# First feed-forward product of a decoder layer, by 2x2x2 blocks with seven products in fifteen of its sixteen column groups

## The chip, the cores and the metric

The kernel runs on one NeuronCore of a Trainium2 chip. The metric is the time of one execution on the device in microseconds (us). The engines are named as the profile names them: PE is TensorE's matrix multiply, PEld its loading of the stationary operand, DVE is VectorE, ACT is ScalarE, POOL is GpSimd, and SP only issues transfers here. POOL issues transfers too.

## What is computed

One decoder layer over 512 tokens of 2048 channels, in float32. Only the part around the change is kept here; the token mixers before it produce `mix`.

```python
x = layer_norm(DEEPNORM_ALPHA * x + mix, ln_mix_g, ln_mix_b)      # x: 512 x 2048
f = jnp.square(jax.nn.relu(x @ w_ff1)) @ w_ff2                    # w_ff1: 2048 x 8192, w_ff2: 8192 x 2048
x = layer_norm(DEEPNORM_ALPHA * x + f, ln_ff_g, ln_ff_b)
```

## The kernel before

**Three products for one.** Each float32 operand is split into a high and a low part of type fp32r, and each product is made of three: high by high, high by low and low by high. `split` does it with two instructions: ACT writes the high part (tile `wh` for weights), DVE writes source minus high part (tile `wl`). Where the split stands in a helper, all splits have its two lines, L86 (ACT) and L87 (DVE).

```python
    def split(dst_h, dst_l, src):                                        # L85
        nc.scalar.activation(dst_h, src, AF.Copy)                        # L86
        nc.vector.tensor_tensor(dst_l, src, dst_h.bitcast(F32), op=OP.subtract)
```

**Steps and their lead.** All products are a list of steps, each with one load of weights (tile `wr`, 512 KB by SP), one split and its matmuls. `fill(i)`, called ahead of the matmuls of step i, writes the loads and splits up to step i + 2 into the engines' programs. The tiles `wh` and `wl` have three buffers each, so the split of step i + 2 starts when step i - 1 has left PE: the splits lead PE by two steps. Every engine takes its instructions in the order in which the program writes them.

**The first feed-forward product (L146).** Its 8192 columns are done in 16 groups of 512. A group has 8 steps of 24 matmuls; the stationary operand is a 128x128 block of weights, the moving one 512 tokens of the activations (`aH`, `aL`), and four banks of PSUM (`mm`) collect the group. Group 0 is done in two halves of 256 tokens (`F[0]` and `F[1]`), since the second half of the tokens leaves the normalisation later; its 384 matmuls have 256 columns. The side work of the first groups finishes the normalised rows (`ln1_finish`, `y_save`) on DVE and ACT.

**What follows each group (`ff1_evac`, from L493).** ACT copies the four banks out with relu (L524) and squares them in place (L527) into `hpR`. Then `parts(0)` and `parts(1)`, one for each half of the group's tiles, are put into the list `late`, and the first and the second step of the next group take one each. A `parts` is: four sums on DVE (L498) that the second feed-forward product needs, a split of seven blocks into `hpH` (ACT) and `hpL` (DVE), and two transfers to HBM by POOL (`h_parts`, L503). The two `parts` of a group have buffers of their own (tags h1 to h6).

**The second feed-forward product (L615, L660)** reads `h_parts` back (`hop`) and already uses blocks of 2x2x2 with seven products. Its sums of weight blocks are on DVE (L585 to L596). The change leaves it as it is, except for the buffers that it starts with.

## Time and profile before

| | |
|---|---|
| Time, median of 3 runs (lowest to highest) | 2449.92 us (2448.81 to 2450.59) |
| Span of the profiled execution | 2448.5 us |
| PE, DVE, ACT, POOL busy, share of the span | 99%, 53%, 35%, 5% |
| Group 0 of the first feed-forward product, with normalisation work between its matmuls | 1110.0 to 1161.3 us |
| Groups 1 to 15 of the first feed-forward product | 1161.3 to 1814.2 us |
| Second feed-forward product and the end | 1814.2 us to the end |

The profiled execution has no time of its own beside its span; the median of the runs is 1.4 us above that span. Times in the trace count from the first instruction. In the rows below a group of instructions stands as line, engine, operation, output<-input, shape and count, then busy time, mean ns of one, and the idle time of the engine ahead of them with what ended it.

### The profile page before, as it was taken

To read this page: it belongs to the slowest core of one execution; us is meant where nothing else is said; L and a number is where in the kernel's file an instruction comes from. 1 tells how busy PE (TensorE), PEld (TensorE's weight loads), DVE (VectorE), ACT (ScalarE), POOL (GpSimd) and SP (SyncE) were. 2 spreads that over 40 slices of the span, in tenths; PEclk is the share of its full clock that TensorE was granted. 3 is DMA by queue.
4 is the path that set the end of the run, shared out by engine and by line. 5 is a ranking of instruction groups with operands and counts; after the bars stand their busy time and mean duration, and the time that the engine had idled before them with its cause. 6 is when DMAs were issued, how large, how long until landed. Compare 5 with 4: busy or idle time off the path is not lost.

```text
span 2448.5 us, 26732 instructions
## 1 busy us (share of the span) xinstructions
PE 2433.2 (99%) x10936; PEld 2010.9 (82%) x10936; DVE 1303.0 (53%) x1409; ACT 851.9 (35%) x952; POOL 130.7 (5%) x188
## 2 busy tenths in 40 slices
PE   9999999999999999999999999999999999999998
PEld 7888888877788888889888888888888888888886
DVE  4532245555522335356653334343347988889887
ACT  4323321244422222137434333343334333333330
POOL 0000000000000000000110101000021000110000
PEclk9999999999999999999999999999999999999999
DMA  6333333322233333465665645546677457575652
GB/s 217 87 94 99 103 96 95 95 78 78 71 93 97 101 95 116 125 198 167 195 243 166 217 155 196 183 160 210 241 262 261 160 186 240 206 240 168 210 164 94
DMA packets 166842, 383.29 MB, mean 157 GB/s; under 512 B 11200, under 2 KB 12224, under 8 KB 165696
## 3 DMA queue, kind: packets, MB, share of 16 engines
q1 hardware_dynamic: 133408, 257.84, 33.5%
q0 software_dynamic: 30720, 117.45, 13.8%
q10 hardware_dynamic: 2592, 6.29, 0.8%
q8 instruction: 86, 1.41, 0.2%
q14 instruction: 36, 0.29, 0.0%
HBM read 317.58 MB, written 63.96 MB: 156 GB/s over the span
## 4 chain that ended last, share of the span: by engine, by line
PE 97%; DVE 1%; DMA 1%; ACT 0%; issue 0%; SPq 0%; POOLq 0%; DVEq 0%
PE mm L146 71%; PE pp L615 20%; PE pp L660 4%; PE sc L349 1%; PE tp L381 1%; DMA w<-in_w_ff 1%; DVE wl L87 0%; PE tp L373 0%; PE tp L275 0%; PE sc L275 0%; DVE part L621 0%; DMA wr<-in_w_in 0%; PE sc L467 0%; PE tp L467 0%; ACT wh L86 0%
## 5 line engine op out<-in xcount | busy, mean ns | idle before, releaser
L87 DVE TENSOR_TENSOR wl<-wr,wh 128x1024 fp32r<-128x1024 f32 (+1 forms) x348 | 423.3, 1221 | 891.5 <-ACT wh L86 890.9
L146 PE MATMUL mm<-aH,wh 128*128 128x512 f32 (+1 forms) x1984 | 768.8, 387 | 0.8 <-ACT wh L86 0.6
L146 PE MATMUL mm<-aH,wl 128*128 128x512 f32 (+1 forms) x1984 | 759.4, 383 | 0.2 <-DVE wl L87 0.2
L146 PE MATMUL mm<-aL,wh 128*128 128x512 f32 (+1 forms) x1984 | 758.7, 382 | 0.0
L86 ACT ACTIVATE wh<-wr 128x1024 fp32r<-128x1024 f32 (+1 forms) x348 | 367.0, 1055 | 878.2 <-PE mm L146 809.0
L615 PE MATMUL pp<-wh,hop 128*128 128x512 f32 x1568 | 483.1, 389 | 0.7 <-ACT hpR L524 0.7
L146 PEld LDWEIGHTS mm<-aH,wh 128*128 128x128 f32 x1984 | 373.2, 188 | 76.4 <-ACT wh L86 2.3
L146 PEld LDWEIGHTS mm<-aL,wh 128*128 128x128 f32 x1984 | 373.2, 188 | 74.3 <-issue 1.9
L146 PEld LDWEIGHTS mm<-aH,wl 128*128 128x128 f32 x1984 | 373.0, 188 | 73.9 <-DVE wl L87 1.1
L615 PEld LDWEIGHTS pp<-wh,hop 128*128 128x128 f32 x1568 | 294.4, 188 | 62.0 <-ACT hpR L524 1.1
L86 ACT ACTIVATE wh<-w 128x1024 fp32r<-128x1024 f32 x196 | 208.1, 1062 | 313.6 <-PE pp L615 295.5
L615 PE MATMUL pp<-wl,hop 128*128 128x512 f32 x784 | 305.2, 389 | 1.0 <-DVE wl L87 1.0
L87 DVE TENSOR_TENSOR wl<-w,wh 128x1024 fp32r<-128x1024 f32 x196 | 238.4, 1222 | 71.4 <-ACT wh L86 64.3
L615 PEld LDWEIGHTS pp<-wl,hop 128*128 128x128 f32 x784 | 147.2, 188 | 32.4 <-DVE wl L87 1.9
L146 PE MATMUL mm<-wh,aH 128*128 128x512 f32 x384 | 149.9, 390 | 0.0
L146 PE MATMUL mm<-wl,aH 128*128 128x512 f32 x384 | 149.5, 389 | 0.0
L146 PE MATMUL mm<-wh,aL 128*128 128x512 f32 x384 | 149.5, 389 | 0.0
L621 DVE TENSOR_TENSOR part<-part,pp 128x1024 f32<-128x1024 f32 x92 | 112.1, 1218 | 12.7 <-PE pp L615 12.7
L87 DVE TENSOR_TENSOR hpL<-hpR,hpH 128x1792 fp32r<-128x1792 f32 (+1 forms) x30 | 61.3, 2044 | 52.1 <-ACT hpH L86 52.1
L146 PEld LDWEIGHTS mm<-wl,aH 128*128 128x128 f32 x384 | 72.1, 188 | 15.2 <-DVE wl L87 0.4
L146 PEld LDWEIGHTS mm<-wh,aL 128*128 128x128 f32 x384 | 72.1, 188 | 15.1
L146 PEld LDWEIGHTS mm<-wh,aH 128*128 128x128 f32 x384 | 72.1, 188 | 14.7
(143 smaller groups left out, 1700.1 us busy)
## 6 DMA issues: line engine op xcount, KB each, us to landing
wr<-in_w_ff SPq DMA_DIRECT2D x152, 512.0 KB, 3.9
wr<-in_w_in SPq DMA_DIRECT2D x127, 512.0 KB, 3.7
w<-in_w_ff SPq DMA_DIRECT2D x112, 512.0 KB, 6.1
hop<-h_parts POOLq DMA_DIRECT2D x98, 512.0 KB, 7.2
h_parts<-hpH POOLq DMA_DIRECT2D x28, 896.0 KB, 5.7
h_parts<-hpL POOLq DMA_DIRECT2D x28, 896.0 KB, 7.7
wr<-in_w_out SPq DMA_DIRECT2D x40, 512.0 KB, 3.7
wr<-in_w_branch_pool SPq DMA_DIRECT2D x16, 512.0 KB, 3.6
```

The lines of the kernel that those rows point to most:

```text
L86: nc.scalar.activation(dst_h, src, AF.Copy)
L87: nc.vector.tensor_tensor(dst_l, src, dst_h.bitcast(F32), op=OP.subtract)
L146: nc.tensor.matmul(o, l, r, start=first and j == 0, stop=last and j == 2)
L349: nc.tensor.matmul(p[:, :n], qT[h][:, qb * P:(qb + 1) * P], kT[h][:, :n], start=True, stop=True)
L381: nc.tensor.matmul(p[:, k * P:], vt["v"][:, k, h * HD:(h + 1) * HD], pT[h][:, k, k * P:], start=k == 0, stop=k == 3)
L615: nc.tensor.matmul(u.ps[:, t], l, r, start=q + j == 0, stop=q == 3 and j == 2)
L621: nc.vector.tensor_tensor(p, p, u.ps, op=OP.add)
L660: nc.tensor.matmul(o, l, r, start=first and i == 0, stop=last and i == 2)
```

## The change

Groups 1 to 15 are no longer steps of 512 tokens by 512 columns. Each is a unit (`FUnit`) of seven products of half the tokens (256), half the 2048 channels and half the 512 columns (M1 to M7), in the order M1 M2 M5 M3 M6 M7 M4, in group 1 M1 M5 M6 M3 M7 M2 M4. A product is two pieces (`FPiece`, numbered j = 0 to 13), a piece is one split of 128x1024 and 24 matmuls with 256 moving columns (L646). A unit has 14 pieces with 336 matmuls, where a group had 8 steps with 192. The split keeps its two instructions (now L89 and L90).

The weights of a unit are four blocks of 1 MB (`w1`), loaded by SP. Four times in a unit one block is added to another in place, 128x2048, on POOL (`W_ADD`, L608): after M1's split the block that M5 reads, after M5's those that M6 and M7 read, after M6's the one that M4 reads. The sums of the activations (`P1` to `P4`) are made once, by `y_sums` and `y_p3`, on DVE and ACT around the second half of group 0.

Three banks of PSUM serve a unit. M3 accumulates on M5's bank after M5's result has been copied out, M6 on M1's, M7 on the same bank after a copy of M1 + M6, and M4 on it after DVE has read it for a block. `hpR` and `hpH` have one buffer each. What followed a group (now `h_parts_out`) is still taken from `late` by the next unit's first two pieces. The finished normalised rows, before on DVE and ACT, are made by POOL in 16 chunks (`y_rows`): after piece 2 of units 1 to 9, and after piece 8 of units 1 to 7. The core of the diff:

```diff
+    W_ADD = nc.gpsimd.tensor_tensor
...
+            nc.gpsimd.dma_start(y_norm[t], acc[t])
...
+    def y_add(out, a, b, op):
+        nc.vector.tensor_tensor(yr[out], yr[a], yr[b], op=op)
+
+    def y_sum(name, src):
+        h = L2["p"].tile([P, 8, 256], F32R, name="ysH", tag=SUM[name][0])
+        l = L2["p"].tile([P, 8, 256], F32R, name="ysL", tag=SUM[name][1])
+        if name == "P2":
+            nc.scalar.activation(h, yr[src], AF.Copy, scale=-1.0)
+            nc.vector.scalar_tensor_tensor(l, yr[src], -1.0, h.bitcast(F32), op0=OP.mult, op1=OP.subtract)
+        else:
+            split(h, l, yr[src])
+        sums[name] = (h, l)
...
+    def y_sums():
+        return [lambda: (y_add("22", "22", "21", OP.subtract), y_sum("P1", "22")),
+                lambda: (y_add("21", "11", "21", OP.subtract), y_add("11", "11", "22", OP.add)),
+                lambda: (y_add("12", "11", "12", OP.subtract), y_sum("P2", "11")),
+                lambda: y_sum("P4", "12")]
...
+    def y_rows(t, n):
+        c = slice(n * 512, (n + 1) * 512)
+        v, g, b = low["u"][:, 1], low["g"][:, 0], low["g"][:, 1]
+        tt = nc.gpsimd.tensor_tensor
+        nc.gpsimd.dma_start(v, y_norm[t, :, c])
+        nc.gpsimd.dma_start(g, bcast(ln_mix_g, c))
+        nc.gpsimd.dma_start(b, bcast(ln_mix_b, c))
+        tt(v, v, g, op=OP.mult)
+        tt(v, v, b, op=OP.add)
+        nc.gpsimd.tensor_scalar(v, v, ALPHA, None, op0=OP.mult)
+        if t >= 2 and n % 2:
+            nc.gpsimd.dma_start(g, y_parts[t - 2, :, c])
+            tt(v, v, g, op=OP.subtract)
+        nc.gpsimd.dma_start(y_parts[t, :, c], v)
...
+    def h_parts_out(g, j):
+        r = R[g][:, j]
+        for d, x0, x1, op in ((4, 0, 2, OP.add), (5, 4, 1, OP.subtract), (6, 1, 0, OP.subtract), (7, 3, 5, OP.subtract)):
+            nc.vector.tensor_tensor(r[:, d], r[:, x0], r[:, x1], op=op)
+        h = L2["p"].tile([P, 7, 256], F32R, name="hpH", tag="t10")
+        split(h, r[:, 1:], r[:, 1:])
+        for e, v in enumerate((h.bitcast(F32), r[:, 1:])):
+            nc.gpsimd.dma_start(h_parts[g // 2, e, :, :, 2 * (g % 2) + j].rearrange("s p f -> p s f"), v)
...
-        def parts(j):
-            a, b, c = ("h1", "h2", "h3") if j else ("h4", "h5", "h6")
-            r = R[j]
-            for d, x0, x1, op in ((4, 0, 2, OP.add), (5, 4, 1, OP.subtract), (6, 1, 0, OP.subtract), (7, 3, 5, OP.subtract)):
-                nc.vector.tensor_tensor(r[:, d], r[:, x0], r[:, x1], op=op)
-            h = L2["p"].tile([P, 7, 256], F32R, name="hpH", tag=b)
-            l = L2["p"].tile([P, 7, 256], F32R, name="hpL", tag=c)
-            split(h, l, r[:, 1:])
-            for e, v in enumerate((h, l)):
-                nc.gpsimd.dma_start(h_parts[g // 2, e, :, :, 2 * (g % 2) + j].rearrange("s p f -> p s f"), v.bitcast(F32))
...
+    ORDER = ("M1", "M2", "M5", "M3", "M6", "M7", "M4")
+    ORDER1 = ("M1", "M5", "M6", "M3", "M7", "M2", "M4")
+    FACTORS = {"M1": ("11", "11"), "M5": ("P1", "11"), "M6": ("P2", "11"), "M3": ("P4", "22"), "M7": ("P3", "12"),
+               "M2": ("12", "21"), "M4": ("22", "11")}
...
+        def get(self, role):
+            self.b[role] = L2["p"].tile([P, 8, 256], F32, name="w1", tag=self.tag[role])
+            k, c0 = int(role[0]) - 1, self.g * 512 + (int(role[1]) - 1) * 256
+            nc.sync.dma_start(self.b[role], w_ff1[k * 1024:(k + 1) * 1024, c0:c0 + 256].rearrange("(a p) n -> p a n", p=P))
+
+        def sum(self, role, other):
+            W_ADD(self.b[role], self.b[role], self.b[other], op=OP.add)
+
+        def give(self, role, new):
+            self.next.tag[new] = self.tag[role]
+            self.next.get(new)
...
+        def split(self):
+            u, j, b = self.u, self.j, self.u.b
+            self.h = G.tile([P, 4, 256], F32R, name="wh", bufs=3)
+            self.l = G.tile([P, 4, 256], F32R, name="wl", bufs=3)
+            split(self.h, self.l, b[FACTORS[self.what][1]][:, 4 * (j % 2):4 * (j % 2) + 4])
+            if j % 2:
+                for o, i in {"M1": (("11", "12"),), "M5": (("11", "22"),), "M6": (("11", "21"),)}.get(self.what, ()):
+                    u.sum(o, i)
+            elif self.what == "M3":
+                u.sum("12", "22")
+            if j in (7, 9, 11, 13):
+                u.give(u.freed[j // 2 - 3], u.order[j // 2 - 3])
+
+        def mult(self):
+            u, what = self.u, self.what
+            if self.j % 2 == 0 and what in ("M1", "M5", "M2"):
+                u.ps[what] = PS.tile([P, 512], F32, name="mm", bufs=6)
+            p = u.ps[{"M3": "M5", "M2": "M2", "M5": "M5"}.get(what, "M1")]
+            for n in range(2):
+                o = p[:, n * 256:(n + 1) * 256]
+                for k in range(4):
+                    ah, al = yblock(FACTORS[what][0], 4 * (self.j % 2) + k)
+                    wh, wl = (v[:, k, n * P:(n + 1) * P] for v in (self.h, self.l))
+                    for i, (l, r) in enumerate(((wh, ah), (wh, al), (wl, ah))):
+                        first = what in ("M1", "M5", "M2") and self.j % 2 + n + k + i == 0
+                        nc.tensor.matmul(o, l, r, start=first, stop=self.j % 2 == 1 and k == 3 and i == 2,
+                                         skip_group_check=True)
+            if self.j % 2:
+                self.evac()
+
+        def evac(self):
+            u, what, ps = self.u, self.what, self.u.ps
+            v = {m: p.rearrange("p (n t) -> p n t", n=2) for m, p in ps.items()}
+            m1, m5, u2 = low["m"][:, 0], low["m"][:, 1], low["u"][:, 0]
+            tt, act = nc.vector.tensor_tensor, nc.scalar.activation
+
+            def block(slot, in0, in1, op):
+                r = R[u.g][:, :, slot]
+                tt(r, in0.rearrange("p (n t) -> p n t", n=2), in1, op=op)
+                act(r, r, AF.Relu)
+
+            if what == "M1":
+                act(m1, ps["M1"], AF.Copy)
+            elif what == "M5":
+                act(m5, ps["M5"], AF.Copy, scale=-1.0)
+            elif what == "M6":
+                act(u2, ps["M1"], AF.Copy, scale=-1.0)
+            elif what == "M3":
+                h_rows(u.g)
+            elif what == "M7":
+                block(3, m5, v["M1"], OP.subtract)
+            elif what == "M4":
+                act(R[u.g][:, :, 1], v["M1"], AF.Relu)
+                act(R[u.g][:, :, :4], R[u.g][:, :, :4], AF.Square)
+                late.extend(h_out(u.g))
+            if what == ("M2" if u.g == 1 else "M3"):
+                block(0, m1, v["M2"], OP.add)
+            if what == ("M3" if u.g == 1 else "M6"):
+                block(2, u2, v["M5"], OP.subtract)
...
-    F += [add(cols(w_ff1, n * 512), 16, "ws", yact, ff1_evac(n)) for n in range(1, 16)]
+    funits = [FUnit(g) for g in range(1, 16)]
...
+    chunks = [(t, n) for n in range(4) for t in (0, 2, 1, 3)]
+    for p in fpieces:
+        fill(pos[2])
+        if late:
+            late.pop(0)()
+        if p.u is funits[0] and p.j == 0:
+            y_p3()
+            funits[0].get("21")
+        p.mult()
+        pos[2] += 1
+        if p.j == 2 and chunks:
+            y_rows(*chunks.pop(0))
+        elif p.j == 8 and chunks and p.u.g < 8:
+            y_rows(*chunks.pop(0))
```

The first place that the prediction speaks of is ACT's program from the end of one group to the next. In it `hpH` is the high part of the sums of the hidden layer, `wh` that of weights, and a name in brackets is an engine or a transfer (DMASW: issued by POOL) that the instruction waits for. Before:

```order
L527 ACTIVATE hpR<-hpR 128x512 [waits Activation_49]
L86 ACTIVATE wh<-wr 128x1024 [waits DMAHW5_49,DVE_49]
L86 ACTIVATE hpH<-hpR 128x1792 [waits DMASW0_49,DVE_49,Activation_49]
L86 ACTIVATE wh<-wr 128x1024 [waits DMAHW6_49,PE_49]
L86 ACTIVATE hpH<-hpR 128x1792 [waits DMASW2_49,DVE_49,Activation_49]
L86 ACTIVATE wh<-wr 128x1024 [waits DMAHW7_49,PE_49]
```

With the change, from one unit to the next:

```order
L673 ACTIVATE hpR<-mm 128x2x256 [waits PE_49]
L674 ACTIVATE hpR<-hpR 128x2x1024 [waits Activation_49]
L89 ACTIVATE wh<-w_10807 128x1024 [waits DMAHW7_49]
L89 ACTIVATE hpH<-hpR 128x1792 [waits DMASW0_49,DVE_49,Activation_49]
L89 ACTIVATE wh<-w_10807 128x1024 [waits PE_49]
L89 ACTIVATE hpH<-hpR 128x1792 [waits DMASW3_49,DVE_49,Activation_49]
L663 ACTIVATE low<-mm 128x512 [waits PE_49]
L89 ACTIVATE wh<-w_10747 128x1024 [waits Pool_49]
```

The order is the same, but the splits between the two `hpH` are now those of pieces 2 and 3 and the next that of piece 4, and the four squares are one instruction. The `wh` of the last row waits for POOL's sum.

The second place is DVE's program over the same stretch, where `wl` is the low part of weights. Before:

```order
L87 TENSOR_TENSOR wl<-wr,wh 128x1024
L498 TENSOR_TENSOR hpR<-hpR 128x256 x4
L87 TENSOR_TENSOR hpL<-hpR,hpH 128x1792
L87 TENSOR_TENSOR wl<-wr,wh 128x1024 x7
L498 TENSOR_TENSOR hpR<-hpR 128x256 x4
```

With the change:

```order
L90 TENSOR_TENSOR wl<-w_10807,wh 128x1024
L543 TENSOR_TENSOR hpR<-hpR 128x256 x4
L90 TENSOR_TENSOR hpR<-hpR,hpH 128x1792
L90 TENSOR_TENSOR wl<-w_10807,wh 128x1024
L543 TENSOR_TENSOR hpR<-hpR 128x256 x4
L90 TENSOR_TENSOR hpR<-hpR,hpH 128x1792
L90 TENSOR_TENSOR wl<-w_10747,wh 128x1024 x2
```

The rows are the same work in the same order, with one split between two lots of sums; the low parts now go back into `hpR`.

The third place is POOL's program in one of units 2 to 9. Before, POOL had only the transfers of a group:

```order
L503 DMA h_parts<-hpH 128x7x256
L503 DMA h_parts<-hpL 128x7x256
L503 DMA h_parts<-hpH 128x7x256
L503 DMA h_parts<-hpL 128x7x256
L503 DMA h_parts<-hpH 128x7x256
```

With the change, from the transfers of the last unit's hidden layer to the sum that M6 reads (the first L608 row of these; the second is the one that M7 reads):

```order
L547 DMA h_parts<-hpH 128x7x256
L547 DMA h_parts<-hpR 128x7x256
L522 DMA low<-y_norm 128x512
L523 DMA low<-in_ln_mix_g 128x512
L524 DMA low<-in_ln_mix_b 128x512
L525 TENSOR_TENSOR low<-low 128x512
L526 TENSOR_TENSOR low<-low 128x512
L527 TENSOR_SCALAR low<-low 128x512
L531 DMA y_parts<-low 128x512
L608 TENSOR_TENSOR w_9845<-w_9845,w_10034 128x2048
L608 TENSOR_TENSOR w_9973<-w_9973,w_10034 128x2048
```

The chunk of normalised rows stands between the hidden layer's transfers and the sum, so the sum comes after both on POOL.

## Rows read from the trace of the kernel before

**Rows 1.** Page of the whole execution: busy time by engine, and the chain that ended last.

```profile
PE 2433.2 (99%) x10936; PEld 2010.9 (82%) x10936; DVE 1303.0 (53%) x1409; ACT 851.9 (35%) x952; POOL 130.7 (5%) x188
PE 97%; DVE 1%; DMA 1%; ACT 0%; issue 0%; SPq 0%; POOLq 0%; DVEq 0%
```

**Rows 2.** Windows, groups 1 to 15: length, busy us (instructions) by engine, granted clock, DMA.

```profile
core 0: us, PE busy (x) PEld busy (x) DVE busy (x) ACT busy (x) POOL busy (x), PEclk, DMA share, GB/s
1161.33:1814.16 652.83, 652.83 (x2882) 540.37 (x2880) 262.36 (x273) 241.13 (x273) 65.02 (x72) 1.00 0.60 200
```

**Rows 3.** Waits of PE, whole execution: us in total, times, longest us.

```profile
PE mm L749 <- DVE warm L746: 1.2, 1, 1.2
PE mm L146 <- ACT wh L86: 0.6, 1, 0.6
PE mm L146 <- DVE wl L87: 0.2, 1, 0.2
```

**Rows 4.** Timeline of PE in group 0, 256 columns: start us, us, instruction.

```profile
1111.08 0.28 PE L146 MATMUL mm<-aH,wh 128*128 128x256 f32 x1
...
1112.76 0.28 PE L146 MATMUL mm<-aH,wl 128*128 128x256 f32 x1
```

**Rows 5.** Timeline of PE in group 6, 512 columns.

```profile
1395.06 0.39 PE L146 MATMUL mm<-aH,wl 128*128 128x512 f32 x1
...
1399.82 0.39 PE L146 MATMUL mm<-aH,wl 128*128 128x512 f32 x1
```

**Rows 6.** Timeline of ACT after a group's end, in brackets the idle time before.

```profile
1381.74 1.05 ACT L86 ACTIVATE wh<-wr 128x1024 fp32r<-128x1024 f32 x1
1385.60 1.70 ACT L86 ACTIVATE hpH<-hpR 128x1792 fp32r<-128x1792 f32 x1 [2.81 <-issue]
1387.21 1.04 ACT L86 ACTIVATE wh<-wr 128x1024 fp32r<-128x1024 f32 x1
1392.05 1.70 ACT L86 ACTIVATE hpH<-hpR 128x1792 fp32r<-128x1792 f32 x1 [3.80 <-issue]
```

**Rows 7.** Timeline of DVE over the same stretch.

```profile
1382.82 1.23 DVE L87 TENSOR_TENSOR wl<-wr,wh 128x1024 fp32r<-128x1024 f32 x1 [7.00 <-ACT wh L86]
1383.96 1.55 DVE L498 TENSOR_TENSOR hpR<-hpR 128x256 f32<-128x256 f32 x4
1387.34 2.03 DVE L87 TENSOR_TENSOR hpL<-hpR,hpH 128x1792 fp32r<-128x1792 f32 x1 [1.82 <-ACT hpH L86]
1389.28 1.22 DVE L87 TENSOR_TENSOR wl<-wr,wh 128x1024 fp32r<-128x1024 f32 x1
```

**Rows 8.** Groups of ACT instructions: busy us, mean ns of one, idle before.

```profile
L86 ACT ACTIVATE wh<-wr 128x1024 fp32r<-128x1024 f32 x346 | 365.8, 1057 | 878.1 <-PE mm L146 809.0 <-DMA wr<-in_w_ff 27.2 <-PE pp L660 21.9
L524 ACT ACTIVATE hpR<-mm 128x512 f32<-128x512 f32 x64 | 36.4, 597 | 43.3 <-PE mm L146 43.3
L809 ACT ACTIVATE ln<-ln 128x2048 f32<-128x2048 f32 x2 | 3.8, 1900 | 0.0
```

**Rows 9.** Groups of DVE instructions.

```profile
L87 DVE TENSOR_TENSOR wl<-wr,wh 128x1024 fp32r<-128x1024 f32 x346 | 421.9, 1224 | 891.4 <-ACT wh L86 890.9
L585 DVE TENSOR_TENSOR w<-w,w 128x2048 f32<-128x2048 f32 x14 | 32.0, 2285 | 2.2 <-DMA w<-in_w_ff 2.2
L87 DVE TENSOR_TENSOR aL<-rl,aH 128x512 fp32r<-128x512 f32 x16 | 11.1, 691 | 12.3 <-ACT aH L86 12.3
L449 DVE TENSOR_SCALAR mv<-mv 128x1 f32<-128x1 f32 x8 | 1.2, 153 | 0.3
```

**Rows 10.** Groups of POOL instructions; DMA_DIRECT2D is the issue of a transfer.

```profile
L541 POOL DMA_DIRECT2D hop<-h_parts x98 | 52.3, 552 | 406.0 <-PE pp L615 399.1 <-issue 7.0
L503 POOL DMA_DIRECT2D h_parts<-hpH x28 | 27.8, 993 | 533.0 <-ACT hpH L86 533.0
L450 POOL TENSOR_TENSOR mv<-mv,nh 128x1 f32<-128x1 f32 x8 | 9.8, 1228 | 1202.4 <-DVE mv L449 1202.4
```

**Rows 11.** Transfers by POOL: count, KB each, median us from issue to landing.

```profile
h_parts<-hpH POOLq DMA_DIRECT2D x28, 896.0 KB, 5.7
h_parts<-hpL POOLq DMA_DIRECT2D x28, 896.0 KB, 7.7
```

More of the change, by code (lines that the diff above doesn't have):

```diff
@@ new lines, in y_p3 @@
+    def y_p3():
+        for c in range(2):
+            split(yH[c][:, :, 256:], yL[c][:, :, 256:], yr["21"][:, 4 * c:4 * c + 4])
+    def y_rows(t, n):
[12 more added lines that the diff above has]
+        nc.gpsimd.dma_start(y_parts[t, :, c], v)
@@ L637, in tail_load @@
         elif m < 6:
-            rest[m] = L2["p"].tile([P, DM], F32, name="ln", tag=f"h{m}")
+            rest[m] = L2["p"].tile([P, DM], F32, name="ln", tag=HOP[m])
             nc.gpsimd.dma_start(rest[m], bcast(ln_ff_g if m == 4 else ln_ff_b))
@@ L729, in decoder_layer @@
     ends = [Last(j) for j in range(16)]
-    steps += pieces + ends
+    steps += fpieces + pieces + ends
     TA, TB, TC = [None], [None], [None]
```

135 lines of the change are left out of this document (76 added, 59 removed).

## The prediction

> **What bounds the kernel now.** I read the page first: PE is busy for 99% of the span, and the chain that ended last is 97% PE [rows 1]. Then the list of PE's waits: none of its entries is over 1.2 us in total, and in the first feed-forward product PE waits 0.2 us for a low part [rows 3]. So the time is the number of matmuls times their spacing, as long as ACT and DVE deliver the splits. In groups 1 to 15 PE is busy for all of 652.83 us, at a granted clock of 1.00 (2.4 GHz); DVE has 262 us of work there, ACT 241, POOL 65 [rows 2]. These engines have room on average. What I looked for is whether they have it at the moment when PE needs them.
>
> **Matmuls.** 512 columns: 21 starts from 1395.06 to 1399.82, 0.2267 us each [rows 5]; 192 of them make a group of 43.5 us. 256 columns: 14 starts from 1111.08 to 1112.76, 0.120 each [rows 4], not half of 0.2267 but 6% more. A unit has 336: 40.3 us, and a piece of 24 takes 2.88. The change saves 3.2 us a unit, 48 in 15 units. That is little for seven products in place of eight, and all that follows is set against it.
>
> **The hidden layer's sums between the splits.** This is the large term. Before, the two lots of sums stand between splits on both engines, and each pass is a chain through them: `wl`, four sums, `hpH` on ACT, `hpL`, the next `wl`. From one `wl` to the next it takes 6.46 us (1382.82 to 1389.28 [rows 7]), with ACT idle for 2.81 and 3.80 us ahead of `hpH` [rows 6]. A step lasts 5.44 us (43.5 / 8), so two passes fall 2 us behind, and the lead of the splits hides it. With the change the passes stand between the splits of pieces 2, 3 and 4, as the order shows, and a piece lasts 2.88 us. I count from the start of a unit's piece 0, with durations from rows 6 to 8:
> ACT can read the last bank at 0.2 (a 256-column matmul lasts 0.28, 0.16 past the next start [rows 4]); relu 0.6 to 0.8, squares of 2048 elements 1.9 to 2.7; `wh` of piece 2 1.06 to 3.8; `wl` 1.22 to 5.0; sums 1.55 to 6.55; `hpH` 1.70 to 8.25; `hpL` 2.03 to 10.3; `wl` of piece 3 to 11.5. Piece 3 starts at 8.64 and wants `wl` at its third matmul, 8.9: PE waits 2.6 us. Next come sums to 13.05. The second `hpH` now writes the buffer that the first transfer still reads; that lands 5.7 us after its issue [rows 11], at 13.95, so `hpH` ends at 15.65, the copy of M1 at 16.25, `wh` of piece 4 at 17.3, `hpL` at 17.7 and `wl` of piece 4 at 18.9. It is due at 11.52 + 0.24 + 2.6 = 14.4: PE waits another 4.5 us. The later splits catch up. 7.1 us, behind groups 0 to 13, so in 14 units: **+99**. A hand-over between engines costs 0.03 to 0.1 us more (1385.51 to 1385.60 [rows 6, 7]); with some ten of them 0.5 us a unit, **+8**.
>
> **Banks of PSUM.** M3, M7 and M4 must wait until the result before them has been read from the bank: two copies by ACT of 0.60 us [rows 8], one DVE instruction of 0.69 [rows 9], each 0.16 after PE's last start. That is 0.76 + 0.76 + 0.85 = 2.4 us a unit, **+35**. Nothing hides it: PE has no other matmul in its program.
>
> **Sums on POOL.** No row shows POOL at a wide addition. From below it is DVE's 2.29 us for 128x2048 [rows 9]. From above, POOL takes 1.228 us for one column where DVE takes 0.153 for a small one [rows 9, 10]; eight times 2.29 is 18.3. A one-column instruction is nearly all fixed cost, so I take the wide row plus the difference of the fixed costs, 1.08: 3.4 us a sum, and 0.69 + 1.08 = 1.8 for 512 columns. Four sums, 13.5 us, fit into a unit, and each has a product between its split and its use. The sum that M6 reads can start at about 20, after piece 5's split, so without a chunk of rows it ends in time for piece 8.
>
> The Trainium skill (GPSIMD Engine Reference, Performance versus the Vector engine) gives 4497 ns for a 2048-element float32 addition on GpSimd and 2293 on VectorE. The trace agrees with the second (2285 ns [rows 9]) and shows nothing of the first; by it each sum ends 1.1 us later, and my estimate of the total would be some 9 us higher.
>
> **Chunks of normalised rows.** In units 2 to 9 a chunk stands on POOL ahead of that sum. POOL issues the second `hpL` at 17.7, and it lands 7.7 us later [rows 11], at 25.4; the chunk's three loads come behind it on the same queue, so I take them as landed at 26. Three instructions of 1.8 make 31.4, an issue of 0.55 [rows 10] 31.9, the sum 35.3, then `wh` and `wl` of piece 8 37.6. It is due at 23.04 + 0.24 + 7.1 + 0.8 = 31.2: 6.4 us late, 8 times: **+51**. At DVE's prices it would be 3.4 us less each time. Off DVE and ACT go the old `ln1_finish` and its relatives; they were covered, so that gains nothing.
>
> **The edges.** `y_sums` puts four additions and three low parts of 128x2048 on DVE, 7 x 2.29 = 16 us, into the last five steps of 2.88 that also need five `wl` of 1.22: 22 us in 14.4, less a lead of 3.5 (two pieces less the 2.3 us of a split), 4 us late. `y_p3` adds two `wl`, 2.4. In group 1 two sums have no product between split and use: 3.4 + 1.06 + 1.22 - 2.88 = 2.8 each, and its chunk costs like the others, 6.4. At the other end, group 15's squares, split and transfers stand in the second product's first splits: about 6. Together **+25**.
>
> **The clock.** Rows 3 show no idle time of PE above 1.2 us in total, and in groups 1 to 15 the granted clock is 1.00 [rows 2]. The change makes idle times of 4.5 and 6.4 us. If the clock falls to 1.2 GHz in one, the next matmuls take twice as long; for one piece that is 2.9 us. Between nothing and 22 such idle times (64 us) I take the 8 longest: **+23**. The Trainium skill (TensorE: Matmul & The Clock Gate, HAM oscillation — how this bites in real kernels) says that waits inside a matmul loop throttle PE again. No row here shows it.
>
> **Sum.** -48 + 99 + 8 + 35 + 51 + 25 + 23 = +193 on a span of 2448.5, or 2641; with the 1.4 us that the median lies above the span, **2643 us**, 8% slower.
>
> **Rivals.**
> 1. The forecast: the two passes hold the splits back. For it speaks that the chain of 6.46 us is a row, and that the engines take their work in order. Its own range, with POOL's price from 2.29 up and the clock term from 0 to 64, is 2590 to 2700. Chance 0.68.
> 2. POOL becomes the bound. From 20, after piece 5's split, three sums S follow each other, and M4's split (piece 12) needs the third by 34.6 + 9.5 - 2.3 = 41.8: above S = 7.2 POOL decides in every unit, and with a chunk far sooner. At S = 8 with chunks of 4 each instruction the sum that M6 reads ends at 26 + 12 + 0.6 + 8 = 46.6, some 11 us later than above, in 8 units +90, and 2 in the rest: 2740 to 2850. For it: the upper bound of the price. The Trainium skill (GPSIMD Engine Reference, Key points) has GpSimd share its SBUF interfaces with VectorE and contend with instructions of two SBUF inputs; `wl`, `hpL` and the sums are all such, and no row shows both at work. Against: on average 13.5 us of sums and 24 us of DVE work fit one after the other into 50. Chance 0.17.
> 3. Not slower: the lead hides the passes as it does now. Two passes would have to fit into two pieces and the lead, 5.76 + 3.5, so 4.6 us each in place of 6.46. For it: PE waits for nothing today although the passes are longer than a step [rows 3]. Then POOL's part is also covered, and -48 + 35 + 10 of the edges give 2447. Chance 0.08.
> 4. Faster: the banks are also free in time and PE runs dense, -48: 2402. Against: a matmul on a bank must follow the copy. Chance 0.03.
> 5. The passes cost half (the second `hpH` finds its buffer free, or POOL's loads land earlier): 2530 to 2590. Chance 0.04.
>
> **Numbers.** The range reaches from the fifth case to the lower half of the second, 2545 to 2770; outside lie cases 3 and 4 and the upper part of 2, about 0.18. A measurement of this kernel can tell 0.2%, 5 us, from no change. Slower is 0.89 from cases 1, 2 and 5; case 3 gives 0.06 to no change and 0.02 to faster, case 4 0.03 to faster.
>
> **What would show it.** Matmuls of 256 columns 0.120 apart inside a piece. PE waits for DVE `wl` (L90) at pieces 3 and 4 of each unit, 2.6 and 4.5 us, and at piece 8 in units 2 to 9; three waits of 0.8 for ACT's copies and DVE's block. Units of some 50 us from 10 on, 57 before. A second `hpH` that starts when the transfer lands. I am wrong if PE stays at 99% there, if the waits for POOL's L608 outweigh those for DVE, or if the clock falls and stays low through whole units.

## The result and the profile after

The changed kernel takes 2726.68 us (2724.10 to 2728.37, 4 runs), the kernel before beside it 2450.26: a ratio of 1.1123, 95% interval 1.1107 to 1.1139. The forecast of slower was right and the time is inside the range of 2545 to 2770, but 84 us above the number, and 27 above the 2590 to 2700 that the forecast gave its own case: it lies between that case and the second rival's.

The profiled span is 2722.3 us, 273.8 more than before. Units 1 to 15 take 917.7 in place of the 652.83 of [rows 2]; they begin 8 us later, and the second product with the end takes 1 us more. First the windows of all units and of the plain unit 12 (no chunk of rows near it), with the columns of [rows 2]:

```profile
1169.30:2087.00 917.70, 704.50 (x5042) 677.91 (x5040) 501.29 (x402) 354.50 (x370) 462.57 (x252) 0.88 0.49 154
1856.50:1908.40 51.90, 45.03 (x338) 43.63 (x337) 32.53 (x28) 23.20 (x24) 24.03 (x9) 0.93 0.48 152
```

No engine is busy all the time. PE, which had no idle time there, is idle for 213 us, and its granted clock is 0.88 in place of 1.00. POOL went from 65 to 463 us. PE's waits in the units, which answer to [rows 3]:

```profile
PE mm L646 <- ACT wh L89: 96.1, 36, 9.6
PE mm L646 <- DVE wl L90: 81.7, 43, 4.6
PE mm L646 <- DVE hpR L659: 16.0, 14, 4.6
PE mm L646 <- ACT low L665: 9.6, 14, 0.7
PE mm L646 <- ACT low L667: 9.6, 14, 0.7
```

The last three are the banks. The first two are splits. Where `wh` itself was late, ACT's own waits say what held it (left out here are its waits for PE, for a buffer or a result, and for DVE's blocks):

```profile
ACT wh L89 <- POOL w L608: 106.5, 11, 14.6
ACT hpH L89 <- issue: 59.7, 13, 8.5
ACT hpH L89 <- DMA h_parts<-hpH: 57.9, 13, 7.0
```

The sums of weight blocks on POOL first, then the two passes: the first `hpH` after its four sums ("issue" stands for a wait that the view can't attach), the second for the transfer that still reads its buffer.

Unit by unit, from the starts of the 5040 matmuls of L646: 75.7 us in the first, 63.6 to 68.4 in units 2 to 9 (they have chunks of rows), 51.9 to 53.2 in 10 to 14, 49.3 in the last. The plain unit is the forecast's: its pieces last 2.9, 2.9, 3.9, 7.4, 6.0, 3.7, 3.0, 2.9, 2.9, 3.7, 3.0, 3.9, 2.9, 2.9 us, so the time over 2.88 stands at pieces 2 to 4 and behind M5, M6 and M7. (A wait of PE is given from here on as the distance between two starts less the usual 0.12; one ahead of a piece's first matmul shows in the length of the piece before.) Its passes in the timeline, ACT first and then DVE, which answer to [rows 6, 7]:

```profile
1887.38 1.70 ACT L89 ACTIVATE hpH<-hpR 128x1792 fp32r<-128x1792 f32 x1 [3.30 <-issue]
1888.98 1.04 ACT L89 ACTIVATE wh<-w 128x1024 fp32r<-128x1024 f32 x1
1894.26 1.70 ACT L89 ACTIVATE hpH<-hpR 128x1792 fp32r<-128x1792 f32 x1 [4.24 <-DMA h_parts<-hpH]
...
1885.75 1.54 DVE L543 TENSOR_TENSOR hpR<-hpR 128x256 f32<-128x256 f32 x4
1889.11 2.02 DVE L90 TENSOR_TENSOR hpR<-hpR,hpH 128x1792 f32<-128x1792 f32 x1 [1.82 <-ACT hpH L89]
1891.05 1.22 DVE L90 TENSOR_TENSOR wl<-w,wh 128x1024 fp32r<-128x1024 f32 x1
1892.19 1.55 DVE L543 TENSOR_TENSOR hpR<-hpR 128x256 f32<-128x256 f32 x4
1895.99 2.03 DVE L90 TENSOR_TENSOR hpR<-hpR,hpH 128x1792 f32<-128x1792 f32 x1 [2.25 <-ACT hpH L89]
```

The unit begins at 1880.4: `hpH` ends at 8.7 (forecast 8.25), the second at 15.6 (15.65), and its `hpL` at 17.6 (17.7). PE's first matmul on the low part of piece 3 starts at 11.9, on that of piece 4 at 18.8; the forecast had these low parts at 11.5 and 18.9.

The surprise is a unit with chunks. Unit 5 begins at 1442.0. POOL first, then DVE, ACT, and one matmul of PE:

```profile
1446.55 4.88 POOL L608 TENSOR_TENSOR w<-w,w 128x2048 f32<-128x2048 f32 x1
...
1465.97 0.54 POOL L524 DMA_DIRECT2D low<-in_ln_mix_b  x1
1472.38 1.28 POOL L525 TENSOR_TENSOR low<-low 128x512 f32<-128x512 f32 x1 [5.88 <-DMA low<-in_ln_mix_g]
...
1476.91 0.61 POOL L531 DMA_DIRECT2D y_parts<-low  x1 [0.30 <-POOL low L527]
1477.55 4.53 POOL L608 TENSOR_TENSOR w<-w,w 128x2048 f32<-128x2048 f32 x1
1482.03 4.51 POOL L608 TENSOR_TENSOR w<-w,w 128x2048 f32<-128x2048 f32 x1
...
1446.89 4.83 DVE L543 TENSOR_TENSOR hpR<-hpR 128x256 f32<-128x256 f32 x1
1451.75 1.09 DVE L543 TENSOR_TENSOR hpR<-hpR 128x256 f32<-128x256 f32 x3
...
1483.20 4.44 DVE L90 TENSOR_TENSOR wl<-w,wh 128x1024 fp32r<-128x1024 f32 x1 [12.00 <-ACT wh L89]
1487.56 1.21 DVE L90 TENSOR_TENSOR wl<-w,wh 128x1024 fp32r<-128x1024 f32 x1
...
1452.93 1.70 ACT L89 ACTIVATE hpH<-hpR 128x1792 fp32r<-128x1792 f32 x1 [7.21 <-issue]
...
1482.11 2.00 ACT L89 ACTIVATE wh<-w 128x1024 fp32r<-128x1024 f32 x2 [9.42 <-POOL w L608]
...
1487.69 0.58 PE L646 MATMUL mm<-ysH,wl 128*128 128x256 f32 x1 [3.68 <-DVE wl L90]
```

Read them by time, in us from the unit's start. The unit before has a chunk behind its piece 8, which puts this unit's first sum on POOL at 4.5. The first of the four small sums on DVE begins 0.3 later and lasts 4.83 us, where such a sum takes 0.42 alone: it ends 0.3 after POOL's sum, and the other three take 1.09 together. So `hpH` comes 3.9 later than in unit 12 (10.9 in place of 7.0), and the loads of piece 2's chunk, which stand behind the pass's last transfer, are issued only from 22.8. The chunk runs from 30.4 to 35.5, the sum that M6 reads to 40.1, and ACT, which waited 9.4 for it, hands over at 41.2. There the next sum is on POOL, from 1482.03 to 1486.54. The low part that PE needs takes 4.44 in place of 1.22 and ends 1.1 after that sum, at 45.6, when the next one takes its usual 1.21. It was due at 31.2 and forecast for 37.6. Of the 15.3 us that this unit takes more than unit 12, 11 stand at pieces 7 and 8 and 4 at piece 2.

The two long rows on DVE are not a slower VectorE: the instruction waits until POOL's has ended, and the trace counts that wait as its own time. In the changed kernel 52 low parts of 128x1024 begin while POOL adds or multiplies two tiles. All 52 end 1.08 to 1.09 us after that instruction of POOL; alone, such a low part takes 1.22.

### The profile page after: what moved, and what is told of

It reads as the page before. It is cut to its first block, busy times and chain, and to the rows that moved or that the text cites. A ratio compares the mean times of both kernels' runs of the same rounds, so it can differ in the third digit from the quotient of the medians.

```text
span 2722.3 us, 31556 instructions
## 1 busy us (share of the span) xinstructions
PE 2487.1 (91%) x13096; PEld 2149.4 (79%) x13096; DVE 1552.6 (57%) x1541; ACT 965.6 (35%) x1045; POOL 529.8 (19%) x368
## 3 DMA queue, kind: packets, MB, share of 16 engines
q0 software_dynamic: 36160, 135.28, 14.8%
## 5 line engine op out<-in xcount | busy, mean ns | idle before, releaser
L90 DVE TENSOR_TENSOR wl<-w,wh 128x1024 fp32r<-128x1024 f32 x406 | 588.4, 1464 | 404.2 <-ACT wh L89 403.9
L89 ACT ACTIVATE wh<-w 128x1024 fp32r<-128x1024 f32 x406 | 424.3, 1055 | 536.3 <-PE pp L764 295.0
L90 DVE TENSOR_TENSOR wl<-wr,wh 128x1024 fp32r<-128x1024 f32 (+1 forms) x228 | 277.5, 1220 | 567.7 <-ACT wh L89 567.2
L89 ACT ACTIVATE wh<-wr 128x1024 fp32r<-128x1024 f32 (+1 forms) x228 | 240.4, 1055 | 612.8 <-PE mm L149 567.1
L149 PE MATMUL mm<-aH,wh 128*128 128x512 f32 (+1 forms) x1024 | 395.8, 386 | 1.3 <-ACT wh L89 1.3
L149 PE MATMUL mm<-aH,wl 128*128 128x512 f32 (+1 forms) x1024 | 386.7, 378 | 5.1 <-DVE wl L90 5.1
L149 PE MATMUL mm<-aL,wh 128*128 128x512 f32 (+1 forms) x1024 | 385.8, 377 | 0.0
L646 PE MATMUL mm<-aH,wh 128*128 128x256 f32 x960 | 286.2, 298 | 57.7 <-ACT wh L89 32.1
L608 POOL TENSOR_TENSOR w<-w,w 128x2048 f32<-128x2048 f32 x60 | 283.9, 4742 | 199.4 <-DVE wl L90 159.1
L646 PE MATMUL mm<-aH,wl 128*128 128x256 f32 x960 | 284.8, 297 | 32.6 <-DVE wl L90 32.6
L646 PE MATMUL mm<-ysH,wh 128*128 128x256 f32 x720 | 228.6, 317 | 73.7 <-ACT wh L89 64.0
L646 PE MATMUL mm<-aL,wh 128*128 128x256 f32 x960 | 281.7, 293 | 0.0
L646 PE MATMUL mm<-ysH,wl 128*128 128x256 f32 x720 | 226.7, 315 | 49.1 <-DVE wl L90 49.1
L646 PEld LDWEIGHTS mm<-aH,wh 128*128 128x128 f32 x960 | 195.0, 203 | 65.8 <-ACT wh L89 35.0
L646 PEld LDWEIGHTS mm<-aH,wl 128*128 128x128 f32 x960 | 195.0, 203 | 36.9 <-DVE wl L90 36.9
L646 PEld LDWEIGHTS mm<-ysH,wh 128*128 128x128 f32 x720 | 159.4, 221 | 81.8 <-ACT wh L89 69.3
```

The lines of the kernel that those rows point to most:

```text
L149: nc.tensor.matmul(o, l, r, start=first and j == 0, stop=last and j == 2)
L608: W_ADD(self.b[role], self.b[role], self.b[other], op=OP.add)
L646: nc.tensor.matmul(o, l, r, start=first, stop=self.j % 2 == 1 and k == 3 and i == 2, skip_group_check=True)
```

## The experiments

Two theories at first. **A**, the record's: the passes hold every unit, the chunk ahead of M6's sum holds units 2 to 9. **B**: GpSimd is the cause, by its price and by what it does to VectorE. The texts put on record ahead of each run say what either expects, with further rivals. Each ratio is to the kernel before, its 95% interval in brackets.

**Sums of weight blocks on VectorE.**

```diff
-    W_ADD = nc.gpsimd.tensor_tensor
+    W_ADD = nc.vector.tensor_tensor
```

> The sums of weight blocks go to VectorE; nothing else changes. The trace of the changed kernel has units of 64 to 68 us with a chunk of rows (2 to 9) and 52 without (10 to 14), and a sum of 4.74 us on POOL. Theory A (the record's: two passes of the hidden layer between the splits hold every unit, and the chunk's loads ahead of the sum on POOL hold units 2 to 9): the second cause goes, the first stays. Units 2 to 9 fall to 51 to 53, units 10 to 14 to 50 to 52, since a sum is 2.3 us on VectorE and no longer beside another engine's; total 2570 to 2600. Rival B (GpSimd is the whole cause, by its price and by what it does to VectorE beside it): all units fall to 43 to 45 and the total to about 2470. Rival C (VectorE, given 9.2 us more work a unit, becomes late itself): units stay at 55 or above, total over 2640.

Measured: 2578.53 us, 1.0526 [1.0508, 1.0543]. Units 2 to 14 take 50.2 to 52.5, with or without a chunk, the first 59.7. So 148 us went with the sums' move off POOL, and 128 are something else. A gave both numbers; B as the whole cause and C fall.

**The chunk moved, sums on POOL as in the change.**

```diff
-        if p.j == 2 and chunks:
+        if p.j == 2 and p.u.g < 3:
             y_rows(*chunks.pop(0))
-        elif p.j == 8 and chunks and p.u.g < 8:
+        elif p.j == 8 and p.u.g < 15:
```

> The sums stay on GpSimd; the chunk of normalised rows is issued behind piece 8 of units 1 to 14, behind the sum that M6 reads, in place of behind piece 2 (only units 1 and 2 have one there too). Theory A: the waits at pieces 7 and 8 go in units 3 to 9, which fall from 66 to 52 to 55; units 10 to 14, which now have a chunk, stay at 52 to 55; total about 2600 to 2630. Rival B (what costs is not the order but that a chunk and the sums share GpSimd and its memory port with VectorE): a unit with a chunk stays 8 us or more above one without, now in units 1 to 14, and the total stays at 2700 or above.

Measured: 2665.28 us, 1.0873 [1.0857, 1.0889]. In units 3 to 9 the waits at pieces 7 and 8 are gone but for 0.8 us in two of them, as A says. But units 3 to 14 take 53.5 to 57.0, over the 52 to 55, and the total is 35 above A's upper end: a chunk behind piece 8, which the record priced at nothing, costs about 3 us in the next unit, at its pieces 2 and 3. The mean of `wl` between 1230 and 1900 us is now 1873 ns, since many wait for an addition on POOL. B's total of 2700 or above does not come, and A's is too low: the order on POOL's queue counts, and so does DVE's waiting for POOL.

**Both edits.**

> Both edits: sums on VectorE and chunks behind piece 8. Theory A: GpSimd then has nothing that PE waits for, and what is left is the two passes, the banks and the clock: units of 50 to 52 throughout, total 2565 to 2590, within 10 us of the kernel with the sums on VectorE alone. Of the 265 us by which units 1 to 15 grew, some 130 to 150 go. Rival B (GpSimd whole cause): units of 43 to 45, total 2470.

Measured: 2581.59 us, 1.0535 [1.0519, 1.0551], 3 us from the first experiment and its interval overlapping: once the sums are off POOL, the place of a chunk is worth nothing. Of the 145 us between the changed kernel and this one, 61 went with the chunk's place and 84 with the engine of the sums. This kernel is the base of the next three. PE's waits for splits in it:

```profile
PE mm L646 <- DVE wl L90: 45.0, 31, 2.1
PE mm L646 <- ACT wh L89: 24.3, 29, 3.1
```

**Without the passes.** The kernel leaves out the sums and splits of the hidden layer and sends what is there.

```diff
-        for d, x0, x1, op in ((4, 0, 2, OP.add), (5, 4, 1, OP.subtract), ...
-            nc.vector.tensor_tensor(r[:, d], r[:, x0], r[:, x1], op=op)
-        h = L2["p"].tile([P, 7, 256], F32R, name="hpH", tag="t10")
-        split(h, r[:, 1:], r[:, 1:])
-        for e, v in enumerate((h.bitcast(F32), r[:, 1:])):
-            nc.gpsimd.dma_start(h_parts[g // 2, e, :, :, 2 * (g % 2) + j]...
+        for e in range(2):
+            for d, v in ((slice(0, 4), r[:, :4]), (slice(4, 7), r[:, 1:4])):
+                nc.gpsimd.dma_start(h_parts[g // 2, e, d, :, 2 * (g % 2) + j]...
```

> As the kernel with both edits, and without the two passes: the four sums and the split of the hidden layer's parts are left out, and the parts that are there are sent as they are, so the result is not the reference's. Theory A (the passes hold the splits of pieces 3 and 4 and nothing else does): the waits at pieces 3 and 4 go, 7 to 8.6 us a unit, and with them most of the intervals at the low clock; units of 43 to 45 (40.3 of matmuls, 2.4 of bank waits, the rest for the clock), total 2465 to 2490. Rival D (the clock, lowered by the bank waits too, and VectorE's sums hold the units): units of 47 or more, total over 2520.

Measured: 2470.78 us, 1.0081 [1.0066, 1.0096], 110.8 less than with them. Of units 2 to 15 all but one take 43.3 to 43.5 us, and the window of units 2 to 14 and most of the last has a granted clock of 1.00, with the three bank waits still there:

```profile
1227.00:1833.00 606.00, 573.32 (x4694) 565.03 (x4693) 407.07 (x295) 283.25 (x309) 209.71 (x226) 1.00 0.69 212
```

A is right, D falls: with the bank waits of 0.85 to 1.03 us alone the granted clock stays at 1.00 here. 43.3 is 40.3 of matmuls, 2.7 of bank waits and 0.3 for the second starts behind them, and that is as long as the 43.5 of a group before: even with all else hidden, this change in this order gains nothing.

**Filled waits.** The waits at pieces 3 and 4 are 0.56, 1.9, about 1.0 and 1.42 us, then the matmuls stand 0.213 apart in place of 0.120, as in unit 12 of the kernel with both edits, where the granted clock from 1756.8 to 1758.0 is 0.57:

```profile
1756.75 0.42 PE L646 MATMUL mm<-aH,wl 128*128 128x256 f32 x1 [1.75 <-DVE wl L90]
1756.97 0.41 PE L646 MATMUL mm<-aH,wh 128*128 128x256 f32 x1
1757.17 0.41 PE L646 MATMUL mm<-aL,wh 128*128 128x256 f32 x1
```

```diff
+    SPIN = {3: (4, 14), 4: (22, 11)}
...
+            dummy = PS.tile([P, 512], F32, name="tp", bufs=1) if spin else None
...
+                        if spin and n + k == 0 and i != 1:
+                            for _ in range(next(spin)):
+                                nc.tensor.matmul(dummy[:, :256], yH[0][:, 0, :P], yH[0][:, 0, :256], start=True, stop=True)
```

> As the kernel with both edits, with matmuls on a spare bank, whose result nobody reads, put into the waits of pieces 3 and 4 of units 2 to 14: 4 ahead of piece 3, 14 ahead of its first low part, 22 and 11 in piece 4 (0.12 us each). In the kernel with both edits some 35 matmuls a unit run at the lower clock behind these waits, 2.9 to 3.7 us a unit, 47 us in all. Theory A1 (PE's idleness lowers the clock, but what is lost in piece 3 is wait again, since piece 4 waits for a split that ends at its own time): the clock stays up, about 1.7 us a unit are saved, those of piece 4; units of 49.5 to 50, total 2553 to 2562. Theory A2 (every slow matmul is on the path): units of 48 to 48.5, total 2535 to 2542. Rival (the clock falls for another reason): units of 51.4 or more, total 2580 or above.

Measured: 2562.13 us, 1.0454 [1.0439, 1.0470], 19.5 less. Units 2 to 14 take 50.0 to 50.9, at A1's upper end and over it. Units 2 to 15, of the kernel with both edits and of this one:

```profile
1228.00:1943.00 715.00, 625.73 (x4701) 606.25 (x4700) 489.21 (x425) 323.28 (x335) 179.32 (x177) 0.93 0.59 181
1228.00:1923.00 695.00, 660.55 (x5365) 647.47 (x5364) 498.64 (x426) 322.03 (x335) 184.50 (x176) 1.00 0.60 186
```

More matmuls in less time. A1 holds: without the idle times the clock stays up. The matmuls' spacing above 0.120, summed where it is under 0.3, falls from 47 us to 12, and the time by 19.5: of 35 us of slow matmuls 19.5 were on the path. That the rest would have been waited at piece 4 in any case is A1's reading; the 1.7 us a unit that it forecast came out as 1.5.

**Own banks.** The results of M3, M6, M7 and M4 no longer add to the product before, so the kernel leaves those sums out.

```diff
-            if self.j % 2 == 0 and what in ("M1", "M5", "M2"):
+            if self.j % 2 == 0:
...
-            p = u.ps[{"M3": "M5", "M2": "M2", "M5": "M5"}.get(what, "M1")]
+            p = u.ps[what]
```

> As the kernel with both edits; M3, M6, M7 and M4 each begin a bank of their own and no longer add to the product before them, so the results of these are left out of the sums and the output is not the reference's. The waits at pieces 5, 9 and 11 (0.85, 0.85, 1.03 us, with three matmuls' slack 2.7 a unit) go. Theory A (nothing hides them): 2.7 to 3.0 us a unit, units of 48.4 to 48.8 and 40.4 to 40.8 in unit 15, total 2537 to 2545. Rival (the time comes back in the waits for splits, since the splits behind the passes are what is late): units stay at 51, total 2570 or above.

Measured: 2545.23 us, 1.0386 [1.0369, 1.0404], 36.4 less, or 2.6 in each of units 2 to 15; the first unit's order has no such wait. Units 2 to 14 take 48.4 to 50.3. The last unit, which has no passes ahead of it, takes 40.4: the matmuls alone. Theory A on the mechanism; the total is 0.2 above its range, and some units are up to 1.5 above theirs.

**Reordered.** One order for all units, in which no product follows one on its bank; sums by halves; passes in seven steps (the order of loads and the places of R's blocks go with it).

```diff
-    ORDER = ("M1", "M2", "M5", "M3", "M6", "M7", "M4")
+    ORDER = ("M1", "M5", "M6", "M3", "M7", "M2", "M4")
...
-            W_ADD(self.b[role], self.b[role], self.b[other], op=OP.add)
+            r, o = (self.b[v][:, 4 * k:4 * k + 4] for v in (role, other))
+            W_ADD(r, r, o, op=OP.add)
...
+        return [lambda: h_parts_out(g, 0), lambda: h_high(g, 0), lambda: h_low(g, 0),
+                lambda: h_parts_out(g, 1), lambda: None, lambda: h_high(g, 1), lambda: h_low(g, 1)] if g < 14 else ...
```

> As the kernel with both edits, with all units in the order M1 M5 M6 M3 M7 M2 M4 (a product never follows one on the same bank), weight sums by halves on VectorE behind each split, and the passes of the hidden layer cut into seven steps over pieces 0 to 6, with a piece between a transfer and the next high part. Theory A (passes in one piece and banks are what is left): bank waits gone, waits for splits 2 to 5 us a unit because VectorE has some 3.4 us of work a piece in pieces 3 to 6; units of 43 to 46, clock at 1.00 in units 2 to 15, total 2475 to 2505. Rival (work on VectorE and ScalarE, not its place, is the bound): units of 49 or more, total 2550 or above.

Measured: 2514.90 us, 1.0267 [1.0251, 1.0282]. The rival falls: eleven units take 42.1 to 45.3, about as A says, but the total is 10 over A's range. Units 1, 2, 10 and 13 take 66.7, 56.4, 49.3 and 51.5: PE waits at piece 11 and behind it, because DVE's block can't write R until a transfer has read it:

```profile
DVE hpR L668 <- DMA h_parts<-hpR: 53.8, 12, 12.4
```

**Small sums on POOL.**

```diff
-            nc.vector.tensor_tensor(r[:, d], r[:, x0], r[:, x1], op=op)
+            nc.gpsimd.tensor_tensor(r[:, d], r[:, x0], r[:, x1], op=op)
```

> As the reordered kernel, with the four small sums of each pass, one sum of y and one low part on GpSimd, and one chunk of rows behind piece 9 of each unit. Theory A: GpSimd works beside VectorE at a time when nothing waits for it and takes 3.1 us a unit off VectorE; units of 41.5 to 44, the first 51 to 55, total 2440 to 2465, which is about the kernel before. Rival B (a narrow sum on GpSimd slows VectorE beside it and takes over 1.5 us): units of 45 or more, slower than the reordered kernel without it, total 2500 or above.

Measured: 2584.23 us, 1.0548 [1.0532, 1.0563]: 69 slower than without. Theory A is wrong; rival B is right on the time and on VectorE, not on its price of over 1.5 us. A small sum takes 1369 ns in the mean on POOL (420 to 439 on DVE in the other runs). The two engines take turns, here with low parts and half sums of 128x1024 on DVE that take 1.22 alone, and small sums that take 0.74 alone on POOL:

```profile
1402.10 0.74 POOL L548 TENSOR_TENSOR hpR<-hpR 128x256 f32<-128x256 f32 x1
1402.92 1.61 POOL L548 TENSOR_TENSOR hpR<-hpR 128x256 f32<-128x256 f32 x1
1404.50 1.71 POOL L548 TENSOR_TENSOR hpR<-hpR 128x256 f32<-128x256 f32 x1
...
1403.86 1.76 DVE L90 TENSOR_TENSOR wl<-w,wh 128x1024 fp32r<-128x1024 f32 x1
1405.54 1.75 DVE L622 TENSOR_TENSOR w<-w,w 128x1024 f32<-128x1024 f32 x1
...
1408.89 1.22 DVE L622 TENSOR_TENSOR w<-w,w 128x1024 f32<-128x1024 f32 x1
```

The low part that begins at 1403.86 ends 1.09 after POOL's sum of 1402.92 has ended. DVE's waits at R for transfers also grew, from 53.8 to 75.3 us. The chunks' new place, one sum of y and its low part on POOL are in this run as well. How the 69 divide was not tried.

**Late blocks, two versions.**

```diff
             elif what == "M7":
+                tt(m5, m5, ps["M1"], op=OP.subtract)
             elif what == "M4":
+                first()
+                second()
+                if u.g == 15:
+                    square()
+                late.extend(([square] if u.g < 15 else []) + h_out(u.g))
```

> As the reordered kernel (sums of weights by halves on VectorE, no product behind one on its bank), with the hidden layer's tile R written only at a unit's last piece (the value of M7's bank goes back into the copy m5 first), the square and the two passes in ten steps over pieces 0 to 9, one chunk of rows behind piece 9 of each unit and two in the last, and of y's sums one and its low part on GpSimd in the first unit. In the reordered kernel PE waited 2.6 us a unit in pieces 4 to 6, where VectorE has sums, low parts and passes at once, and in units 1, 2, 10 and 13 another 4 to 10 us at piece 11, where VectorE waited for the transfer that still reads R. Theory A (where the passes stand, not their work, is the cost): both go, units of 41.5 to 43.5, the first 50 to 56, total 2440 to 2475: the kernel before again, about. Rival (VectorE's work, 497 us of 692 in one kernel here, is too much at this pace): units stay at 44 or more, total 2490 or above.

> As the kernel with late blocks, with a step without work between the sums and the high part and between the second sums and theirs, so that the last transfer of a unit is issued behind piece 10, and the chunk behind piece 11. Theory A: the second high part finds its buffer free, units of 41 to 43, total 2435 to 2470. Rival (the transfer now lands too late for the first block of the next unit's end, and the write of R waits): units of 45 or more.

Measured: 2489.65 us, 1.0161 [1.0147, 1.0175], and 2487.14, 1.0150 [1.0136, 1.0164]. Units 2 to 15 take 40.5 to 45.2 and 40.7 to 46.5, and all fifteen together 658.0 and 656.7 us, against the 652.8 before. All passes are in them, so it is their place and not their work that costs. Both totals are above A's range, for a reason that no theory had: PE stands for 22 to 23 us at the start of the second product. In the first of the two:

```profile
1869.60 2.29 DVE L761 TENSOR_TENSOR w<-w,w 128x2048 f32<-128x2048 f32 x1 [25.62 <-DMA h_rest<-hpH]
...
1839.50 0.54 POOL L531 DMA_DIRECT2D low<-in_ln_mix_b  x1 [1.51 <-DMA hop<-h_parts]
1851.15 1.26 POOL L532 TENSOR_TENSOR low<-low 128x512 f32<-128x512 f32 x1 [11.11 <-DMA low<-in_ln_mix_g]
...
1860.82 0.78 POOL L572 DMA_DIRECT2D h_rest<-hpH  x1
```

The sum on DVE writes the tile that `h_rest` still has to read, and that transfer stands on POOL's queue behind a chunk, whose loads stand behind the loads of the parts.

**The two chunks out of the last unit.**

```diff
-        if p.j == 9 or p.j == 3 and p.u.g == 15:
+        if p.j == 9 and p.u.g < 15 or p.j == 13 and p.u.g in (2, 3):
```

> As the first kernel with late blocks, with the two chunks of rows that stood in the last unit moved behind piece 13 of units 2 and 3. In that kernel PE waited 23 us at the start of the second product for a low part whose sum of blocks on VectorE could not start: its buffer E takes the tile of the hidden layer's high part, still being read by a transfer that stood on GpSimd's queue behind the chunks' loads. Theory A: that wait goes and nothing else changes, total 2463 to 2470, 0.5 to 0.8% above the kernel before. Rival (the transfer is late because of the loads of the parts themselves, which stand on the same queue): total 2483 or above.

Measured: 2479.02 us, 1.0116 [1.0099, 1.0133]. The wait of 23 us is gone (2.0 are left of PE's waits for `wl` there), so A has the cause. The total misses its range by 9: units 3 and 4, behind the moved chunks, take 52.0 and 46.9 where they took 43.0 and 43.1. It is the best version found, and still 1.2% slower than before.

**Work on POOL that nobody waits for.**

```diff
+        if p.j == 12 and 4 <= p.u.g < 14:
+            for i in range(8):
+                nc.gpsimd.tensor_tensor(low["g"][:, 0], low["g"][:, 1], low["g"][:, 1], op=OP.subtract)
```

> As the kernel with both edits (sums on VectorE, chunks behind piece 8, units of 51.4 us), with eight instructions on GpSimd of 128x512 elements each, behind piece 12 of units 4 to 13, that read and write a buffer which nobody needs then; nothing waits for them but the transfers behind them on GpSimd's own queue. They take some 11 us from the unit's end on, beside the four sums and low parts of pieces 2 to 4 of the next unit. Theory B1 (GpSimd slows VectorE beside it: low parts took 2.4 to 2.8 us in the changed kernel where GpSimd summed, 1.22 where not): low parts and sums there take 1.4 times their time or more, units 5 to 14 grow by 1.5 to 5 us, total 2597 to 2630. Rival B2 (only GpSimd's place in the order of the sums counted): VectorE's durations stay, units stay within 0.5 us, total 2578 to 2587.

Measured: 2608.38 us, 1.0648 [1.0630, 1.0665], 26.8 over its base. B1 holds in that VectorE's low parts grow, by 1.6 to 1.7 times, and the total is in its range; B2 falls. It came at another place than meant: POOL is ahead of PE and does it beside pieces 9 to 13, where PE's wait at piece 11 grew from 1.03 us to between 1.8 and 3.3. DVE and POOL here, then DVE at the same place of the base:

```profile
1478.23 1.93 DVE L90 TENSOR_TENSOR wl<-w,wh 128x1024 fp32r<-128x1024 f32 x1 [1.65 <-ACT wh L89]
1480.09 2.06 DVE L90 TENSOR_TENSOR wl<-w,wh 128x1024 fp32r<-128x1024 f32 x1
1482.07 0.67 DVE L659 TENSOR_TENSOR hpR<-low,mm 128x512 f32<-128x512 f32 x1
...
1478.02 1.05 POOL L982 TENSOR_TENSOR low<-low 128x512 f32<-128x512 f32 x1
1479.15 1.91 POOL L982 TENSOR_TENSOR low<-low 128x512 f32<-128x512 f32 x1
1481.14 1.90 POOL L982 TENSOR_TENSOR low<-low 128x512 f32<-128x512 f32 x1
```

```profile
1471.15 2.36 DVE L90 TENSOR_TENSOR wl<-w,wh 128x1024 fp32r<-128x1024 f32 x2 [1.65 <-ACT wh L89]
1473.65 0.69 DVE L659 TENSOR_TENSOR hpR<-low,mm 128x512 f32<-128x512 f32 x1
```

The engines alternate. POOL's first addition ends at 1479.07 and the first `wl` 1.09 later; POOL's second, 1.04 alone, ends 0.9 after that `wl`; the second `wl` ends 1.09 after POOL's second. Each waits for the other's to end. The block, which reads one operand from PSUM, keeps its 0.67 beside POOL's third addition.

## Why the prediction was right, and where its sum was not

**Matmuls, -48: right.** 0.120 apart inside a piece, 40.4 us for a unit with nothing else.

**Passes, 99 and 8 for hand-overs: right.** Taking them out gives 110.8 us, of which the filled waits put 19.5 down to the clock. That leaves 91. The place was right (pieces 3 and 4), the low parts come within 0.5 us of the times forecast, and the second `hpH` starts when the transfer lands. In the plain unit PE waits 5.3 us at pieces 2 to 4, for the forecast 7.1, and loses 3.7 more to slow matmuls: the low parts come at their own times, and a PE that has been slow waits less for them.

**Banks, 35: right.** 36.4, as 2.6 us in 14 units where the sum had 2.4 in 15.

**Clock, 23: near in size, by luck.** The filled waits gave 19.5, in the base without POOL's part. But the clock falls there behind waits of 1 to 2 us in every unit, and the sum had counted eight pieces behind idle times of 4.5 and 6.4. In the changed kernel itself, where the matmuls' loss by the same sum is 68 us, it was not tried.

**Chunk, 51, and group 1's sums and chunk, 12 of the edges: this is the step that failed, by its size.** With the sums off POOL 148 us go: 118 in units 2 to 9 (14.8 each, for the 6.4), 16 in unit 1, 11 in units 10 to 15, the rest outside the units. Three things make it up. The price of a sum: 4.53 us with nothing on DVE beside it (the first of the two in unit 5) and 4.74 in the mean of 60, for the 3.4 taken from a one-column row. The Trainium skill (GPSIMD Engine Reference, Performance versus the Vector engine) has 4497 ns, and here the trace agrees. The overlap: I put POOL's and DVE's instructions beside each other at their own prices, and the rows show them one after the other. The Trainium skill (GPSIMD Engine Reference, Key points) warns of contention, for instructions with two SBUF inputs; the trace agrees, and the last experiment shows it with work that no one waits for. And the chunk behind piece 8 of units 1 to 7, which I had not priced: it pushes the next unit's first sum onto the first pass.

Unit 5 shows all three against the forecast's times. The pass, held by that sum, issues its last transfer late, so the chunk's first instruction starts 4.4 later; its instructions take 1.3 to 1.5 for the 1.8 priced, so it ends 3.6 later; with the dearer sum it is 4.8; and the low part, which waits out the next sum, ends 8.0 later, at 45.6 for 37.6.

The prediction named as a sign of being wrong that the waits for POOL's sums outweigh those for DVE, and that is what came: 148 us went with POOL's sums, 111 with the passes. The forecast's first cause is the second in size, and the time is in the range because the range reached into rival 2's. Rival 2 had the right engine and a wrong place: POOL is no bound by its length (463 us of 918); it holds by the order of its queue and by making DVE wait. What the prediction said against it, that POOL's sums and DVE's work fit one after the other into a unit, is true on average and did not help a low part that was due at once.

**Edges, the other 13.** The first product's units begin 8 us late, as two of the terms said in part (4 and 2.4); unit 1 with sums on DVE is another 8 longer than a later one; the 6 at the start of the second product did not come, it takes 1 us more.

The measured pieces, -48 + 91 + 36 + 20 + 148 + 17, give 264 of the 276 us; 12 are not placed.

**Rival 3**, not slower, was off for this order, but the first product came close to it in the end: with passes, banks and sums all moved, the fifteen units take 657 to 658 us for 652.8. What remains over the kernel before is the first unit (53 to 55 us) and what chunks and transfers do at the ends.
